# A two-block transformer kernel on one core: activations of the first block in rows of 512 columns, and feed-forward tiles at another place in SBUF

## The chip, the cores and the metric

The kernel runs on one core of one Trainium2 chip. The metric is device microseconds (us) of one execution. In the engines' names of the profile, PE is TensorE's matrix products, PEld its loads of the stationary operand, DVE is VectorE, ACT is ScalarE, POOL is GpSimd and SP is SyncE, which issues the weight transfers.

## The reference

512 tokens of 1024 channels go through two blocks, one after the other, in float32. Cut to what matters here:

```
# first block
h = x
h = h + 0.5 * swiglu(rmsnorm(h), ffn1_wg, ffn1_wu, ffn1_wd)   # 1024 -> 2816 -> 1024
u = rmsnorm(h) @ w_in                                         # queries, keys, values, gates
h = h + concat(rmsnorm(nsa(u)), rmsnorm(forgetting(u))) @ w_out
h = h + 0.5 * swiglu(rmsnorm(h), ffn2_wg, ffn2_wu, ffn2_wd)
h = h + sigmoid(rmsnorm(h) @ ple_w_gate) * rmsnorm(p @ ple_w_proj)
# second block: 16 meta tokens are put before the 512
h = concat(meta, h)
proj = rmsnorm(h) @ w_in_2                                    # nine parts of 1024
h = h + merged(hgrn2, gated convolution) @ w_out_2
a, val = split(rmsnorm(h) @ w_up_2)
h = h + (silu(causal_dwconv(a)) * val) @ w_down_2
out = rmsnorm(h)[16:]
```

## The kernel before

Channels lie on the 128 partitions and tokens in the free dimension. `KB` = 8 blocks of 128 channels make the width of 1024, and `FB` = 22 blocks the 2816 hidden channels, worked through in two halves of `HB` = 11. `T2` = 528 is the number of tokens with the meta tokens, `SEQ` = 512 without them.

**A product.** Every float32 operand is split into an upper part and a rest (names that end in h and l, or whi and wlo for weights), both of type float32r. `mm3` makes one block of a product as three instructions: upper times upper, upper weight times rest, rest of the weight times upper. The stationary operand is loaded by a load of its own (PEld) ahead of each product.

**Weights.** `Stream` brings weight chunks of 128 x 1024 in from HBM over SP's queue into `wraw`, and ACT and DVE split them into `whi` and `wlo`. `advance` keeps transfers and splits ahead of the products.

**Dense products.** `pieces_of` runs over the K blocks of one group of products: for each block k it takes 128 columns of a weight chunk as the stationary operand and the row `x[:, k]` of the activations, 512 tokens, as the moving one. In the feed-forward (`ffn`) a hidden block takes two groups of 8 K blocks, gate and up, with the activations of a `Norm` as moving operand. `down_proj` then takes for each of 8 output blocks 11 K blocks, with the hidden tiles `hh` and `hl` as moving operand. The moving operands of the first block are these: `X0` (`x0h`, `x0l`) in the first feed-forward, the output projection and the gate of the embedding; `X1` (`x1h`, `x1l`) in the second feed-forward; `hh` and `hl` in both down projections; `ph`, `pl` in the embedding's own projection. In the projections of the attention the roles are the other way round: 128 tokens of `X0` are stationary and 256 columns of weights move (288 in the first three chunks).

**Tiles.** `X0` and `X1` are tiles of 128 x 8 x 528 for the whole kernel. The first block uses the first 512 of the 528 columns of each row, the second block all of them, mostly in two products of 258 to 264 columns. `hh` and `hl` are taken from a pool that each feed-forward opens for itself. In the second feed-forward the pool gives two scratch tiles (`sq`) before them, since its norm's squares are summed ahead of it. Addresses follow from the order in which tiles are taken.

**Order.** Dense products are issued in program order. Side work (norms, splits, softmax) is issued between them by an estimate of the engines' clocks (`Clocks`). That estimate knows nothing of addresses. All instructions of the compute engines have the same line in the profile, L144, that of the wrapper `Engine`, so rows are told apart by their operands' names. Feed-forward groups write to PSUM banks `b` in the first block, and to `acc` and `h` in the second.

Where the tiles start within each partition of SBUF, taken from the built program of either version, as the remainder of a division by 512 bytes:

| operand | before | after |
|---|---|---|
| `whi`, `wlo`, 128 columns of block k (512 bytes each) | 160 | 160 |
| `x0h`, `x0l`, `x1h`, `x1l` in the first block, row k | 128 + 64 k | 160 |
| `hh`, `hl`, first and third feed-forward, any row | 160 | 160 |
| `hh`, `hl`, second feed-forward, any row | 288 | 160 |
| `ph`, `pl` | 160 | 160 |
| `x1h`, `x1l` in the second block, row k, first token | 128 + 64 k | 160 + 64 k |

Of the kernel before, what the change touches and what calls it, by code (L numbers as in the profile page):

```python
# [16 lines left out]
# The output leaves the meta tokens out: past the recurrence only the last two of them count, which a convolution looks  # L17
# back to, and two more before its own one. Products in two parts want both of them even.
# [6 lines left out]
HB = FB // 2  # L25
# [4 lines left out]
# groups of 256 columns of w_in, with their first columns, in the order of the attention's products  # L30
# [4 lines left out]
# column blocks of the per-channel parameters, in the order they are packed  # L35
# [12 lines left out]
# constants of the first block: cos, sin, causal, cmp mask, rows with a cmp block, head pick  # L48
# [9 lines left out]
class Clocks:  # L58
    """An estimate of when each engine is done with what was issued to it: it decides the order of issue only."""

    ENGINES = ("PE", "DVE", "ACT", "POOL")
    # from the end of an instruction to the start of one that depends on it
# [5 lines left out]
    def __init__(self):  # L68
        self.free = dict.fromkeys(self.ENGINES, 0.0)
        self.hop = {e: np.array([self.HOP.get((f, e), 200.0) for f in self.ENGINES]) for e in self.ENGINES}  # L70
        # per place: end of the last write and of the last read by each engine, for every 32 partitions and element
        self.marks, self.names, self.counts, self.index = {}, {}, {}, {}
        self.last = self.skip = 0.0
        self.dma = 2160.0
# [4 lines left out]
    def turn(self, ap, bufs):  # L79
        """A tile that takes one of `bufs` places in turns with others of its tag."""  # L80
        t = ap.tensor
        n = self.counts[t.tag] = self.counts.get(t.tag, -1) + 1
        self.names[t.name] = t.tag, n % bufs
        return ap
# [16 lines left out]
    def load(self, ap):  # L101
        """A transfer into a tile."""
        m, q, x = self.spot(ap)
        t = max(self.dma, m[:, :, q, x].max() + 1300)
        self.dma = t + 128 * 4 * _free_size(ap) / 360
        m[0, -1, q, x] = self.dma + 800
# [27 lines left out]
class Engine:  # L134
    """An engine whose instructions also move the estimate."""
# [55 lines left out]
class Slots:  # L191
    """Things used in turns (PSUM banks, scratch tiles), each with the estimated time from which it is free."""
# [9 lines left out]
    def get(self, keep=0, low=False):  # L202
        """A slot that is free by now, or None; `keep` of them stay for others."""
# [12 lines left out]
class Stream:  # L216
    """Weight chunks in the order in which they are used: loads run ahead of the split, the split ahead of the products."""
# [48 lines left out]
    def keep(self, j, pool):  # L266
        """The parts of chunk j have a place of their own."""
        self.kept[j] = pool

    def advance(self):  # L270
        """Split up to `ahead` chunks past the last one taken (`held`: taken ones that stay longer), keep the loads running."""
# [20 lines left out]
def build(tc, A, out):  # L292
# [9 lines left out]
    # ------------------------------------------------------------------ weight order  # L302
# [58 lines left out]
    # ------------------------------------------------------------------ what stays for the whole kernel  # L361
    h = base.tile([128, KB, T2], FT, name="h")
    X0 = (base.tile([128, KB, T2], FR, name="x0h"), base.tile([128, KB, T2], FR, name="x0l"))
    X1 = (base.tile([128, KB, T2], FR, name="x1h"), base.tile([128, KB, T2], FR, name="x1l"))
    ssq = base.tile([128, T2], FT, name="ssq")
    rB = base.tile([128, T2], FT, name="rB")
    rtok = base.tile([128, 5], FT, name="rtok")
# [14 lines left out]
    # ------------------------------------------------------------------ side work  # L382
    class Task:
        """Work beside the dense products, in stages: the next one is issued when the last one is done by the estimate."""
# [29 lines left out]
    def force():  # L414
        """Nothing can be issued now: go on to the next moment at which something is done."""
# [24 lines left out]
    class Store:  # L440
        """n tiles of one kind that are taken and given back."""

        def __init__(self, pool, name, n, shape, dt=FT):
            """pool: one for all of them, or a list with one for each."""
# [8 lines left out]
        def drop(self, ids):  # L453
            """Done with some of them."""
# [29 lines left out]
    def act(o, i, fn, exact=False, **kw):  # L484
        """ScalarE function with the table set chosen: Exp and Ln share one unless the logarithm has to be exact."""
# [8 lines left out]
    def mm3(ps, w, x, first, last):  # L494
        """hi*hi + hi*lo + lo*hi of one K block into each (psum, columns) pair."""
# [8 lines left out]
    def run(pieces, ev=None):  # L504
        """A group of products in pieces, with the side work between them; ev takes up the result."""
# [9 lines left out]
    def pieces_of(ps, w, x, ks=range(KB), first=0, last=KB - 1, step=1, off=0):  # L515
        """x: pair of tiles with K blocks, or a list of pairs, one for each K block."""
# [12 lines left out]
    # ------------------------------------------------------------------ rmsnorm  # L529
    def refine(r, v, t, wide=None):  # L530
        """r close to v**-0.5: one Newton step; the result may go, repeated, to a wider tile."""
# [9 lines left out]
    def rsqrt(r, v, t, wide=None):  # L541
        """In stages."""
# [6 lines left out]
    class Norm:  # L549
        """h * gain split into two parts, sums of squares on the side; the row factor rB comes after the products."""  # L550
# [41 lines left out]
    def wide_factors(src, n, dst, banks, pool, tag="sq"):  # L592
        """(mean over channels + eps)**-0.5 on every partition; the sum takes src in two parts."""
# [22 lines left out]
    def row_factors(src, n, r, banks, dst=None, keep_v=None):  # L616
        """(mean over channels + eps)**-0.5, tokens on partitions in r and, where it is asked for, on every partition."""
# [26 lines left out]
    # ------------------------------------------------------------------ gated feed-forward of the first block  # L644
# [7 lines left out]
    def ffn(norm, next_norm, pool, extra=None):  # L652
        n = SEQ
        hh = pool.tile([128, HB, n], FR, name="hh")
        hl = pool.tile([128, HB, n], FR, name="hl")
# [39 lines left out]
        for hf in range(2):  # L695
            for f in range(HB):
                g_ = banks.grab()
                if ws.i == 0:
                    # the first two groups side by side, as their K blocks come in
# [13 lines left out]
    # ================================================================== first block  # L713
# [7 lines left out]
    with tc.tile_pool(name="ffn1", bufs=1) as pool:  # L721
        n0 = Norm("ffn1_norm", META, SEQ, X0, pool)
        nmix = Norm("mix_norm", META, SEQ, X0, pool)
        table("silu_and_others")
        # products that nobody reads: TensorE has its full clock when the first loads are there
# [5 lines left out]
        # the first two chunks of weights come in halves  # L731
# [30 lines left out]
        ffn(n0, nmix, pool)  # L762
        drain()

    # ------------------------------------------------------------------ attention
    with tc.tile_pool(name="att", bufs=1) as pool:
# [16 lines left out]
        def place(dt):  # L783
            """First the windows of the compressed keys, then the outputs of the forgetting attention."""
# [18 lines left out]
        stack_tiles = [t[:, kb, :SEQ] for t in X1 for kb in range(KB)]  # L803
# [4 lines left out]
        def seen(*aps):  # L808
            """Condition: all of these have been written by now."""
            return lambda: all(M.written(a) <= M.now() for a in aps)  # L810

        # ---- values and gates, tokens on partitions
        def ev_aux(bs):
# [17 lines left out]
            # the gates are 1 / (1 + exp(-z))  # L831
# [8 lines left out]
            # log sigmoid(z) = min(z, 0) - log(1 + exp(-|z|)), the logarithm with its rounding put back  # L840
# [21 lines left out]
        def proj_aux():  # L862
            bs = [banks.grab() for _ in range(4)]
            k = 0
            for nk in (3, 3, 2):
                w = ws.get()

                def piece(k, i, w=w):
                    def f():
                        hi, lo = wk(w, i, 288)  # L870
                        for t in range(4):
                            c = slice(t * 128, (t + 1) * 128)
                            for n, (a, b) in enumerate(((X0[0], hi), (X0[0], lo), (X0[1], hi))):
# [6 lines left out]
        def gain_tables():  # L880
            # scores carry the sign -1/8, so that the row maximum is a minimum of what is stored
            for i, (n, f) in enumerate((("q_norm_nsa", -0.125), ("k_norm_slc", 1.0), ("k_norm_win", 1.0),
                                        ("q_norm_fox", -0.125))):
                V.tensor_scalar(cols[:, i:i + 1], pc(n), f, None, op0=OP.mult)
                if i < 3:
                    # the gains of the rotated channels are in the tables of the rotation
# [22 lines left out]
        def proj_half(ev):  # L909
            """256 columns, tokens on partitions; two token blocks share a bank, whose first product clears it for both."""  # L910
            bs = [banks.grab() for _ in range(2)]
            for wi in range(2):
                w = ws.get()

                def piece(k, i, w=w):
                    def f():
                        hi, lo = wk(w, i, 256)
                        for t in range(4):
                            c = slice(t * 128, (t + 1) * 128)
                            d = bs[t // 2].t[:, (t % 2) * 256:(t % 2) * 256 + 256]  # L920
                            for n, (a, b) in enumerate(((X0[0], hi), (X0[0], lo), (X0[1], hi))):
# [6 lines left out]
        # ---- queries and keys: norm and rotation with tokens on partitions, then channels on partitions  # L928
# [9 lines left out]
        def split_q(z, col, r):  # L938
            """Per head the two parts of q, one above the other."""
# [9 lines left out]
        def split_k(z, col, r):  # L949
            """Per head the upper part of k twice and the lower part twice."""  # L950
# [19 lines left out]
        def rotate(z, cos, sin, nh):  # L970
            """The first 16 channels of nh heads."""
# [13 lines left out]
        def qk_half(hz, tables, pairs):  # L985
            """tables: rotation of (first head, heads, table); pairs: what takes up each pair of heads."""
            def g(bs):
# [7 lines left out]
                # the row factor of the norm before cancels against this one, but for eps, which is scaled instead  # L995
# [68 lines left out]
        # ---- softmax attention, one unit = one head and 128 queries  # L1064
# [8 lines left out]
        def unit(u, hp):  # L1073
# [8 lines left out]
            if extra is not None:  # L1082
                # the forget sums of the keys; those of the query are the same along a row and leave its softmax as it is
# [35 lines left out]
        def user(ids, n):  # L1119
            """The slots `ids` are free again after n units have taken their scores."""  # L1120
# [34 lines left out]
        # 16 blocks of 64 keys and a window of 512 keys are all the keys there are, by the shapes alone: the selected and the  # L1155
        # window attention both go over all keys up to the query
        def nsa_units(j):
# [3 lines left out]
            for kind in range(2):  # L1161
                # two pairs of heads share a key: eight units each, twice
# [27 lines left out]
        # ---- compressed keys and values  # L1190
# [1054 lines left out]
```

## Time and profile before

| | |
|---|---|
| median of 3 runs | 2053.38 us (2053.29 to 2054.24) |
| span of the profiled execution, first to last instruction | 2052.2 us |
| PE busy | 2040.9 us, 99% of the span, 14058 instructions |
| PEld busy | 1807.5 us, 88% |
| DVE busy | 1208.6 us, 59% |
| ACT busy | 878.8 us, 43% |
| DMA, mean | 87 GB/s |

Of the profiled execution the trace has the span; what lies around it, as the difference to the median of the other runs, is 1.2 us. The chain of work that ended last is followed back from the last instruction, and its shares tell which engine set the end. A busy PE counts a product from its start to a modelled end, and products overlap; how fast they follow each other is read from a stretch's length over the number of products, or of weight loads, in it.

### The profile page before, as it was taken

The page shows a single profiled execution, that of the slowest core. Times are in us where ns is not written, and L with a number is a line of the kernel's source. Part 1 is how long each engine was busy: PE and PEld are TensorE (multiplying, and loading weights), DVE is VectorE, ACT ScalarE, POOL GpSimd, SP SyncE. Part 2 cuts the span into 40 slices and gives each one's busy share as a digit, 9 for nine tenths or more (in the row PEclk, how much of TensorE's full clock was granted, in tenths as well). Part 3 has the DMA queues.
Part 4 walks back from the last instruction along what each step waited for, and adds up shares of the span by engine and source line. Part 5 has one row for each costly group of instructions (what it writes and reads, how often), then busy time and mean ns, then how long its engine had stood idle before and what let it go on. Part 6 is the DMA issues. An engine that isn't in the chain of part 4 may idle for free.

```text
span 2052.2 us, 33936 instructions
## 1 busy us (share of the span) xinstructions
PE 2040.9 (99%) x14058; PEld 1807.5 (88%) x14058; DVE 1208.6 (59%) x2243; ACT 878.8 (43%) x1513; POOL 6.4 (0%) x17
## 2 busy tenths in 40 slices
PE   9999999999999999999999999999999999999998
PEld 7888888999997888888888999999999999888987
DVE  6433444678874844334458567666666766535554
ACT  5222223467767533223236444555546443222223
POOL 0000000000000000000000000000000000000000
PEclk9999999999999999999999999999999999999999
DMA  5223223332000422332232222222222232233222
GB/s 181 92 83 113 94 79 96 116 115 72 27 17 11 134 93 80 95 113 91 76 111 93 90 84 73 73 84 83 75 82 66 81 103 85 82 102 103 93 75 80
DMA packets 58170, 179.16 MB, mean 87 GB/s; under 512 B 7424, under 2 KB 9728, under 8 KB 58016
## 3 DMA queue, kind: packets, MB, share of 16 engines
q1 hardware_dynamic: 57648, 175.56, 27.3%
q8 instruction: 111, 1.82, 0.3%
q0 software_dynamic: 368, 1.42, 0.2%
q14 instruction: 43, 0.35, 0.1%
HBM read 174.86 MB, written 2.10 MB: 86 GB/s over the span
## 4 chain that ended last, share of the span: by engine, by line
PE 98%; DVE 1%; ACT 1%; DMA 0%; issue 0%; SPq 0%; DVEq 0%
PE b L144 58%; PE acc L144 28%; PE h L144 12%; DVE h L144 0%; DMA wraw<-in_ffn_wg 0%; ACT x1h L144 0%; ACT x1l L144 0%; DVE x1h L144 0%; DVE s L144 0%; ACT AT L144 0%; ACT whi L144 0%; DVE rd L144 0%; ACT L144 0%; ACT s L144 0%; DVE OA L144 0%
## 5 line engine op out<-in xcount | busy, mean ns | idle before, releaser
L144 DVE TENSOR_TENSOR wlo<-wraw,whi 128x1024 fp32r<-128x1024 f32 (+4 forms) x365 | 402.4, 1103 | 326.5 <-ACT whi L144 325.3
L144 ACT ACTIVATE whi<-wraw 128x1024 fp32r<-128x1024 f32 (+4 forms) x364 | 348.0, 961 | 431.0 <-PE h L144 138.5
L144 PE MATMUL acc<-x1h,whi 128*128 128x258 f32 (+2 forms) x1472 | 305.7, 289 | 0.0
L144 PE MATMUL acc<-x1l,whi 128*128 128x258 f32 (+2 forms) x1472 | 296.9, 283 | 0.0
L144 PE MATMUL acc<-x1h,wlo 128*128 128x258 f32 (+2 forms) x1472 | 296.8, 283 | 0.0
L144 PEld LDWEIGHTS acc<-x1h,whi 128*128 128x128 f32 x1472 | 228.5, 189 | 3.7
L144 PEld LDWEIGHTS acc<-x1l,whi 128*128 128x128 f32 x1472 | 228.4, 189 | 0.0
L144 PEld LDWEIGHTS acc<-x1h,wlo 128*128 128x128 f32 x1472 | 227.7, 189 | 0.0
L144 PE MATMUL b<-x0h,whi 128*128 128x512 f32 (+2 forms) x504 | 195.9, 391 | 0.2 <-DVE whi L144 0.2
L144 PE MATMUL b<-x0h,wlo 128*128 128x512 f32 (+2 forms) x504 | 195.2, 390 | 0.0
L144 PE MATMUL b<-x0l,whi 128*128 128x512 f32 (+2 forms) x504 | 195.2, 390 | 0.0
L144 PE MATMUL b<-x1l,whi 128*128 128x512 f32 (+1 forms) x368 | 142.2, 390 | 0.0
L144 PE MATMUL b<-x1h,wlo 128*128 128x512 f32 (+1 forms) x368 | 142.1, 390 | 0.0
L144 PE MATMUL b<-x1h,whi 128*128 128x512 f32 (+1 forms) x368 | 142.1, 390 | 0.0
L144 PE MATMUL b<-hh,wlo 128*128 128x512 f32 x352 | 137.9, 392 | 0.0
L144 PE MATMUL b<-hh,whi 128*128 128x512 f32 x352 | 137.9, 392 | 0.0
L144 PE MATMUL b<-hl,whi 128*128 128x512 f32 x352 | 137.9, 392 | 0.0
L144 ACT ACTIVATE hh<-u 128x512 fp32r<-128x512 f32 x66 | 41.7, 632 | 175.2 <-DVE u L144 175.2
L144 PEld LDWEIGHTS b<-x0h,whi 128*128 128x128 f32 x504 | 94.6, 189 | 22.0 <-ACT x0h L144 0.9
L144 PEld LDWEIGHTS b<-x0l,whi 128*128 128x128 f32 x504 | 95.0, 190 | 21.4 <-DVE x0l L144 0.3
L144 PEld LDWEIGHTS b<-x0h,wlo 128*128 128x128 f32 x504 | 94.6, 189 | 21.1 <-DVE wlo L144 0.3
L144 PE MATMUL b<-whi,x0h 128*128 128x256 f32 (+1 forms) x352 | 101.8, 289 | 0.3 <-DVE x1h L144 0.3
(371 smaller groups left out, 3545.1 us busy)
## 6 DMA issues: line engine op xcount, KB each, us to landing
wraw<-in_w_in SPq DMA_DIRECT2D x72, 512.0 KB, 3.6
wraw<-in_w_up SPq DMA_DIRECT2D x44, 512.0 KB, 3.5
wraw<-in_ffn_wg SPq DMA_DIRECT2D x43, 512.0 KB, 3.5
wraw<-in_ffn_wu SPq DMA_DIRECT2D x43, 512.0 KB, 3.5
wraw<-in_ffn_wd SPq DMA_DIRECT2D x32, 384.0 KB, 3.1
wraw<-in_ffn_wd SPq DMA_DIRECT2D x32, 320.0 KB, 2.9
wraw<-in_w_half SPq DMA_DIRECT2D x20, 512.0 KB, 3.6
wraw<-in_w_down SPq DMA_DIRECT2D x16, 384.0 KB, 3.0
```

The source lines that it names most:

```text
L144: r = f(*a, **k)
```

## The change

Four edits, apart from comments. `rtok`, a tile of 20 bytes, is taken from the pool before `X0` instead of after `rB`, which moves `X0`, `X1`, `ssq` and `rB` up by 32 bytes and nothing behind them. `Y0` and `Y1` are views of the same tiles as `X0` and `X1`, with rows of 512 columns one behind the other; all of the first block uses them in place of the tiles' first 512 columns. The second block keeps `X0` and `X1`. `hidden` takes `hh` and `hl` from the pool before anything else does.

```diff
     h = base.tile([128, KB, T2], FT, name="h")
+    rtok = base.tile([128, 5], FT, name="rtok")
     X0 = (base.tile([128, KB, T2], FR, name="x0h"), base.tile([128, KB, T2], FR, name="x0l"))
     X1 = (base.tile([128, KB, T2], FR, name="x1h"), base.tile([128, KB, T2], FR, name="x1l"))
+
+    Y0, Y1 = (tuple(t.rearrange("p k t -> p (k t)")[:, :KB * SEQ].rearrange("p (k t) -> p k t", k=KB) for t in x)
+              for x in (X0, X1))
     ssq = base.tile([128, T2], FT, name="ssq")
     rB = base.tile([128, T2], FT, name="rB")
-    rtok = base.tile([128, 5], FT, name="rtok")
...
-    def ffn(norm, next_norm, pool, extra=None):
+    def hidden(pool):
+        return pool.tile([128, HB, SEQ], FR, name="hh"), pool.tile([128, HB, SEQ], FR, name="hl")
+    def ffn(norm, next_norm, pool, hid, extra=None):
         n = SEQ
-        hh = pool.tile([128, HB, n], FR, name="hh")
-        hl = pool.tile([128, HB, n], FR, name="hl")
+        hh, hl = hid
...
-        n0 = Norm("ffn1_norm", META, SEQ, X0, pool)
-        nmix = Norm("mix_norm", META, SEQ, X0, pool)
+        hid = hidden(pool)
+        n0 = Norm("ffn1_norm", META, SEQ, Y0, pool)
+        nmix = Norm("mix_norm", META, SEQ, Y0, pool)
...
-        stack_tiles = [t[:, kb, :SEQ] for t in X1 for kb in range(KB)]
+        stack_tiles = [t[:, kb] for t in Y1 for kb in range(KB)]
...
-            run(pieces_of([(b.t, c512)], ws.get(), X0, range(4), 0, 3), ev_out(fb, b))
+            run(pieces_of([(b.t, c512)], ws.get(), Y0, range(4), 0, 3), ev_out(fb, b))
...
-        n2 = Norm("ffn2_norm", META, SEQ, X1, pool)
-        nple = Norm("ple_gate_norm", META, SEQ, X0, pool)
+        hid = hidden(pool)
+        n2 = Norm("ffn2_norm", META, SEQ, Y1, pool)
+        nple = Norm("ple_gate_norm", META, SEQ, Y0, pool)
...
-            run(pieces_of([(b.t, c512)], ws.get(), X0), ev_gate(fb, b))
+            run(pieces_of([(b.t, c512)], ws.get(), Y0), ev_gate(fb, b))
```

The other uses of `X0` in the first block (the projections of the attention, its normed outputs, the second half of the output projection) become `Y0` in the same way. On each engine the built program of the new version has the same instructions in the same order with the same waits as the one before: 12775 on PE, 2245 on DVE, 1467 on ACT, 21 on POOL and 389 on SP, and only addresses in SBUF differ.

## Rows read from the trace of the kernel before

**Rows 1.** The page: span, busy time of the engines, and the chain that ended last.

```profile
span 2052.2 us, 33936 instructions
PE 2040.9 (99%) x14058; PEld 1807.5 (88%) x14058; DVE 1208.6 (59%) x2243; ACT 878.8 (43%) x1513; POOL 6.4 (0%) x17
PE 98%; DVE 1%; ACT 1%; DMA 0%; issue 0%; SPq 0%; DVEq 0%
```

**Rows 2.** Waits of PE: who for whom, us in total, times, longest.

```profile
PE b L144 <- DVE onesr L144: 1.3, 1, 1.3
PE h L144 <- DVE fr L144: 1.3, 1, 1.3
```

**Rows 3.** Stretches of the down projections: length, PEld busy (loads), granted clock, DMA share, GB/s.

```profile
core 0: us, PEld busy (x), PEclk, DMA share, GB/s
131.43:191.28 59.85, 49.56 (x264) 1.00 0.34 105
314.48:374.33 59.85, 49.55 (x264) 1.00 0.34 99
828.09:889.43 61.34, 49.73 (x264) 1.00 0.33 103
1012.02:1073.36 61.34, 49.73 (x264) 1.00 0.35 103
1795.72:1855.58 59.86, 49.57 (x264) 1.00 0.35 105
```

**Rows 4.** Stretches of the first block's products with X0 or X1 moving; columns as before.

```profile
10.80:30.41 19.61, 15.78 (x84) 1.00 0.67 229
30.41:131.43 101.02, 81.68 (x436) 1.00 0.28 89
191.28:314.48 123.20, 99.38 (x528) 1.00 0.28 90
688.20:704.99 16.79, 13.55 (x73) 1.00 0.57 172
704.99:828.09 123.10, 99.52 (x530) 1.00 0.29 91
889.43:1012.02 122.59, 99.13 (x528) 1.00 0.28 91
1095.00:1129.85 34.85, 28.16 (x150) 1.00 0.29 92
```

**Rows 5.** Two stretches of Rows 4, one behind it: busy time of all engines.

```profile
core 0: us, PE busy (x) PEld busy (x) DVE busy (x) ACT busy (x) POOL busy (x), PEclk, DMA share, GB/s
191.28:314.48 123.20, 123.20 (x529) 99.38 (x528) 54.35 (x64) 34.95 (x43) 0.00 (x0) 1.00 0.28 90
1073.36:1129.85 56.49, 56.49 (x245) 45.82 (x244) 48.90 (x67) 36.63 (x55) 0.00 (x0) 1.00 0.29 94
```

**Rows 6.** Timeline of PE at the start: start us, modelled us, operands, shape.

```profile
9.23 0.63 PE L144 MATMUL b<-x0l,whi 128*128 128x512 f32 x1
9.66 0.63 PE L144 MATMUL b<-x0h,wlo 128*128 128x512 f32 x1
```

**Rows 7.** Stretches of 256 columns (attention), 65 columns, and 256 columns from hh.

```profile
389.75:404.06 14.31, 14.31 (x121) 1.00 0.29 87
610.29:613.54 3.25, 3.15 (x29) 1.00 0.00 0
2032.94:2035.81 2.87, 2.87 (x24) 1.00 0.00 0
```

**Rows 8.** Second block, stretches of 258, 258, 264 and 512 columns from X1.

```profile
1149.17:1166.45 17.28, 17.28 (x145) 1.00 0.41 122
1682.12:1687.90 5.78, 5.78 (x48) 1.00 0.39 107
1202.25:1207.56 5.31, 5.17 (x43) 1.00 0.16 59
1676.54:1682.12 5.58, 4.52 (x26) 1.00 0.17 65
```

**Rows 9.** Groups of PE by shape: operands, columns, count, busy us, mean ns.

```profile
L144 PE MATMUL acc<-x1h,whi 128*128 128x258 f32 x992 | 204.8, 288 | 0.0
L144 PE MATMUL b<-whi,x0h 128*128 128x256 f32 x320 | 92.3, 288 | 0.3 <-DVE x1h L144 0.3
L144 PE MATMUL acc<-x1h,whi 128*128 128x260 f32 x256 | 53.1, 289 | 0.0
L144 PE MATMUL acc<-x1h,whi 128*128 128x264 f32 x224 | 47.7, 294 | 0.0
L144 PE MATMUL acc<-x0h,whi 128*128 128x258 f32 x96 | 19.4, 283 | 0.0
```

More of the change, by code (lines that the diff above doesn't have):

```diff
@@ L761, in build @@
         spawn(squares(), 22e3)
-        ffn(n0, nmix, pool)
+        ffn(n0, nmix, pool, hid)
         drain()
@@ L872, in f @@
                             c = slice(t * 128, (t + 1) * 128)
-                            for n, (a, b) in enumerate(((X0[0], hi), (X0[0], lo), (X0[1], hi))):
+                            for n, (a, b) in enumerate(((Y0[0], hi), (Y0[0], lo), (Y0[1], hi))):
                                 P.matmul(bs[t].t[:, :288], a[:, k, c], b, start=k == 0 and n == 0,
@@ L920, in f @@
                             d = bs[t // 2].t[:, (t % 2) * 256:(t % 2) * 256 + 256]
-                            for n, (a, b) in enumerate(((X0[0], hi), (X0[0], lo), (X0[1], hi))):
+                            for n, (a, b) in enumerate(((Y0[0], hi), (Y0[0], lo), (Y0[1], hi))):
                                 P.matmul(d, a[:, k, c], b, start=k == 0 and n == 0 and t % 2 == 0,
@@ L1394, in out_norm @@
             dest[2].add(t)
-        na, normed = ((t[0][:, f:f + 4], t[1][:, f:f + 4], set()) for t, f in ((X0, 0), (X0, 4)))
+        na, normed = ((t[0][:, f:f + 4], t[1][:, f:f + 4], set()) for t, f in ((Y0, 0), (Y0, 4)))
         def nsa_norm(t):
@@ L1454, in build @@
             ws.held = fb
-            run(pieces_of([(half[fb][0].t[:, 256:], slice(256, 512))], half[fb][1], X0, range(4, 8), 4, 7, off=4))
+            run(pieces_of([(half[fb][0].t[:, 256:], slice(256, 512))], half[fb][1], Y0, range(4, 8), 4, 7, off=4))
         wait(lambda: len(normed[2]) == 4)
@@ L1477, in build @@
                 b, w = half[fb]
-                run(pieces_of([(b.t[:, :256], slice(0, 256))], w, X0, range(4, 8), 4, 7, off=4), ev_out(fb, b, n2))
+                run(pieces_of([(b.t[:, :256], slice(0, 256))], w, Y0, range(4, 8), 4, 7, off=4), ev_out(fb, b, n2))
                 ws.held = 0
@@ L1481, in build @@
             b = banks.grab()
-            run(pieces_of([(b.t, c512)], ws.get(), X0, range(4, 8), 4, 7, off=4), ev_out(fb, b, n2))
-        ffn(n2, nple, pool, lambda: (S.activation(ph, pr, AF.Copy), V.tensor_sub(pl, pr, ph.bitcast(FT))))
+            run(pieces_of([(b.t, c512)], ws.get(), Y0, range(4, 8), 4, 7, off=4), ev_out(fb, b, n2))
+        ffn(n2, nple, pool, hid, lambda: (S.activation(ph, pr, AF.Copy), V.tensor_sub(pl, pr, ph.bitcast(FT))))
         drain()
```

## Prediction

> **What bounds the kernel now.** I read the page first, then the waits, then stretches of equal products. The chain that ended last is PE for 98% of the span, and PE is busy for 99% of it [rows 1]. The longest waits of PE are 1.3 us each, one at the start and one at the end [rows 2]. So the time is how fast TensorE's products follow each other, and a change that leaves the instructions, their order and their waits as they are can act on the time only through that pace. The reader is to see it in stretches that hold nothing but one kind of product: length divided by the count of weight loads, one load for each product.
>
> The pace of products of 512 columns is not one number. The two down projections of the first feed-forward take 59.85 us for 264 products, 226.7 ns each; the two of the second take 61.34 us for 264, 232.3 ns; that of the third, in the second block, takes 59.86 us again [rows 3]. These five stretches have the same code, shapes, count and granted clock of 1.00, and nearly the same DMA share. What differs is where `hh` and `hl` begin: remainder 160, that of the weights, in the first and third, and 288 in the second. The products with `X0` or `X1` moving, whose rows begin at 128 + 64 k and so never at 160, go at 232.2 to 233.5 ns in every stretch [rows 4], like the down projections at 288. So the row says: 226.7 ns where the moving operand begins at the weights' remainder, and about 5.6 ns more, at the same clock, where it doesn't.
>
> **The change part by part.** No instruction is added, removed or moved on any engine or queue. I take 226.7 ns for every product of 512 columns in the first block that now begins at 160, and subtract stretch by stretch [rows 3, 4]:
>
> - First feed-forward, first half, as soon as products run at the full clock: 84 products in 19.61 us, 19.04 at the new pace, 0.57 us less; then 435 in 101.02 us (one load of the row's 436 belongs to the product after the edge), 98.61 at the new pace, 2.41 less.
> - Second half: 528 in 123.20 us, 119.70 at the new pace, 3.50 less.
> - Second feed-forward, first half: 530 loads in 123.10 us, two of them the norm's sum, so 528 products at 232.3 ns, 2.94 less. Second half: 528 in 122.59 us, 2.89 less.
> - Its two down projections, once `hh` and `hl` begin at 160: twice 61.34 − 59.85, 2.98 less.
> - Gate of the embedding: 150 in 34.85 us, 232.3 ns, 0.84 less; its other 42 products stand in the same stage and give 0.24 at the same difference. Together 1.09.
> - Output projection: 72 products in 16.79 us, 233.2 ns, 0.47 less; the 96 products of its first half, at the same 6.5 ns, 0.62. Together 1.09.
>
> Sum: 14.49 us from `X0` and `X1`, 2.98 us from `hh`, 17.47 us in all. The products ahead of 10.5 us follow each other 430 ns apart [rows 6], 1.2 columns in a ns, the lower of the clock's two levels (1.2 GHz); no row shows what an address does there, and I count nothing for the dozen of them.
>
> Two kinds of product change their addresses without becoming like those of rows 3. In the attention's projections the activations are stationary and 256 columns of weights move: 3 x 320 products [rows 9], at 119.2 ns (120 in 14.31 us) [rows 7]. Both operands now begin at 160. The nearest row that has this is the last down projection, 256 columns of `hh`: 24 in 2.87 us, 119.6 ns. A bound from below is the stretch of 65 columns, 28 in 3.25 us, 116.1 ns [rows 7]: a product of a quarter of the columns goes hardly faster, so the load of the stationary operand sets the pace here. I take the nearest row, 0.5 ns more with rounding, 0.5 us lost over 960 products; the bounds are 3.0 us gained (116.1 ns) and, by the nearest wider product, 258 columns at 120.4 ns (48 in 5.78 us) [rows 8], 1.2 us lost.
>
> In the second block `X0` and `X1` lie 32 bytes higher. Narrow products, 258 to 264 columns, are 3 x (992 + 256 + 224 + 96) = 4704 [rows 9]. Rows that start at 48 and 56 beyond a multiple of 64 go at 120.0 ns (144 in 17.28 us), those at 0 and 8 at 120.4 ns (48 in 5.78 us) [rows 8]. After the change these classes become 16 and 24, and 32 and 40, all of which keep what the old ones share, a first half on a multiple of 16 bytes and a second 8 bytes off it. I take no change, and 0.4 ns either way, 1.9 us, as the bound. The 528 products of 512 columns there go at 232.5 ns (24 in 5.58 us) from a remainder of 16 + 64 k [rows 8]; at 48 + 64 k they are still not at 160, so nothing is counted.
>
> What hides the rest: DVE is busy for 54.35 of 123.20 us and ACT for 34.95 in the densest stage that gets shorter, DMA for 0.28 [rows 5]. Losing 3.5 us leaves them far from the bound. The tightest stage is the embedding's, DVE 48.90 of 56.49 us [rows 5]; with 1.1 us less it is busy for 88%. If that cover were gone, what would be late is the group of products whose bank DVE has not yet emptied, at a cost of the 1.1 us that the stage gained at most.
>
> Net: 17.47 − 0.5 = 17.0 us. The span of 2052.2 us becomes 2035.2; the median of the runs lies 1.2 us above the span, so **2036.4 us**.
>
> A page speaks against this. The Trainium skill, SBUF — State Buffer, in its section on the two separate sides of SBUF, says that PE never waits on anyone for SBUF, and its table of paths gives the moving operand and the weight load read ports of their own. By that rule the remainder could not matter and the sum would be zero. The trace doesn't agree: 1.49 us between two stretches of 264 like products that differ in the address of one operand [rows 3]; I go by the rows.
>
> **The rivals.** (a) *The place of the activations doesn't work as that of `hh` does.* Only `hh` was seen at both remainders; `X0` and `X1` lie below the weights in a partition, `hh` above them, and eight different remainders of `X0` all give about 232 ns. For it: no row shows an activation of a `Norm` at 160. Against it: the pace at the wrong remainder is the same for `hh` and `X1`, 232.3 ns, which speaks for one mechanism. Then only the 2.98 us come, and 0.5 go: 2050.9 us. Halfway, with half of the 14.49 us, it is 2043.6 us.
>
> (b) *Addresses don't matter*, and the two paces of the down projections come from something else that differs between the feed-forwards, such as what DVE and ACT read and write beside them. That is the page's rule as a mechanism of this kernel. Against it stands that the third feed-forward, with other side work, goes at the pace of the first. Time: 2053.4 us, no change.
>
> (c) *Slower: the second block pays for the 32 bytes.* Its 4704 narrow products are tight to the weight load and more than those that gain. The dearest stretch of them is 264 columns, 42 in 5.31 us, 126.4 ns [rows 8]. If the new addresses bring all of them from 120.4 to that, 6.0 ns each, 28.2 us are lost and the time is 2064.6 us. It decides from 3.6 ns each, where the 17.0 us are used up. Against it: the two classes of starts in rows 8 differ by 0.4 ns, and part of those 126.4 is six more columns and other work between them.
>
> **How the numbers follow.** The forecast has a chance of 0.82: five stretches fix its price, and the layout after the change is that of `hh` in the first feed-forward, row for row. Halfway gets 0.07, (a) 0.04, (b) 0.04, (c) 0.03. The likeliest case's own range is 2036.4 − 3.5 (attention at 116.1 instead of 0.5 lost) − 1.9, that is 2031, up to 2036.4 + 0.7 (attention at 120.4) + 1.9 and 1.3 us for one new wait as long as PE's longest [rows 2], about 2040.5. It holds about 8 in 10, so it is the range. A measurement of this kernel can tell about 0.2%, 4.1 us, from no change. Faster by more than that: forecast and halfway, 0.89. Within: (a) and (b), 0.08. Slower: 0.03.
>
> **What the new profile would show.** Right: the second feed-forward's down projections take 59.85 us each, and the four stretches of 528 products about 119.7 us; the attention's projections stay within 1 ns of 119.2; the stretch of 48 products of 258 columns stays at 5.8 us; PE's waits stay as short as they are. Wrong by (a): the down projections get shorter and the 528 products stay at 122.6 to 123.2 us. By (b): no stretch moves. By (c): the first block gains and the second block, which starts 1129.85 us into the span now, takes over 17 us longer.

## The result

| | before | after |
|---|---|---|
| median of 5 runs | 2053.55 us (2053.29 to 2054.25) | 2038.27 us (2037.52 to 2039.51) |
| ratio, 95% interval | | 0.9924 [0.9913, 0.9934] |
| span of the profiled execution | 2052.2 us | 2037.7 us |

The change makes the kernel faster by 15.3 us by the medians; 17.0 were forecast. The spans of the two profiled executions differ by 14.5 us, since that of the changed kernel (2039.51 us) is the longest of its five. The page of the changed kernel has the same counts as [rows 1], DVE and ACT busy for as long as before, and the difference in PE.

```profile
span 2037.7 us, 33936 instructions
PE 2025.4 (99%) x14058; PEld 1807.2 (89%) x14058; DVE 1209.1 (59%) x2243; ACT 878.7 (43%) x1513; POOL 6.4 (0%) x17
```

The stretches of the down projections after the change, in the order and with the columns of [rows 3] (length, PEld busy and loads, granted clock, DMA share, GB/s):

```profile
129.99:189.82 59.83, 49.55 (x264) 1.00 0.35 105
309.50:369.34 59.84, 49.55 (x264) 1.00 0.34 99
820.47:880.31 59.84, 49.55 (x264) 1.00 0.36 106
999.99:1059.83 59.84, 49.55 (x264) 1.00 0.35 105
1780.96:1840.84 59.88, 49.55 (x264) 1.00 0.36 105
```

All five are alike now: the two in the middle went from 61.34 to 59.84 us. The stretches with `X0` or `X1` moving, which answer to [rows 4] (the fourth here is that of the second feed-forward's first half without its first 33 products):

```profile
31.36:129.99 98.63, 81.65 (x436) 1.00 0.29 91
189.82:309.50 119.68, 99.10 (x528) 1.00 0.31 93
683.94:700.28 16.34, 13.52 (x73) 1.00 0.62 176
708.24:820.47 112.23, 92.91 (x495) 1.00 0.30 90
880.31:999.99 119.68, 99.10 (x528) 1.00 0.30 93
1081.21:1115.22 34.01, 28.15 (x150) 1.00 0.32 94
```

119.68 us over 528 products is 226.7 ns, the pace of the down projections to the tenth of a ns. The attention's first stretch of 256 columns and three stretches of the second block, which answer to [rows 7, 8] (256, 258, 258 and 512 columns):

```profile
384.71:399.18 14.47, 14.47 (x121) 1.00 0.30 94
1134.56:1151.86 17.30, 17.30 (x145) 1.00 0.39 122
1667.10:1672.89 5.79, 5.79 (x48) 1.00 0.45 108
1661.51:1667.10 5.59, 4.51 (x25) 1.00 0.18 71
```

The attention's products lose 0.16 us in 120, and the second block's stay within 0.02 us of what they were.

### The profile page after: what moved, and what is told of

It reads as the page before. It is cut to its first block, busy times and chain, and to the rows that moved or that the text cites. A ratio compares the mean times of both kernels' runs of the same rounds, so it can differ in the third digit from the quotient of the medians.

```text
span 2037.7 us, 33936 instructions
## 1 busy us (share of the span) xinstructions
PE 2025.4 (99%) x14058; PEld 1807.2 (89%) x14058; DVE 1209.1 (59%) x2243; ACT 878.7 (43%) x1513; POOL 6.4 (0%) x17
## 4 chain that ended last, share of the span: by engine, by line
PE 98%; DVE 1%; ACT 1%; DMA 0%; issue 0%; SPq 0%; DVEq 0%
PE b L144 57%; PE acc L144 29%; PE h L144 12%; DMA wraw<-in_ffn_wu 0%; DVE h L144 0%; ACT x1h L144 0%; ACT x1l L144 0%; DVE x1h L144 0%; ACT AT L144 0%; DVE s L144 0%; DVE rd L144 0%; ACT L144 0%; ACT whi L144 0%; ACT s L144 0%; DVE OA L144 0%
```

## The experiments

Theory E, as in the prediction: a product's pace is set by where its two operands begin relative to each other. "Even" is said below of operands that begin at the same remainder. Rivals: what helps is that the rows lie a multiple of 512 bytes apart, or the address 160 itself, or the work beside the products. Runs with one execution are read by their stretches, not by their time, since the start of an execution moves by over 1 us (below).

**Only `hh` and `hl` first in their pools.** The kernel before, with `hid = hidden(pool)` ahead of the norms of either feed-forward, and nothing else of the change.

> The kernel before with one edit: hh and hl are taken from the pool first, so that they begin at 160 in the second feed-forward too; X0 and X1 as before. Theory E: its two down projections take 59.85 us each in place of 61.34, no other stretch moves, 2053.5 - 3.0 = 2050.5 us. Rival (the two paces come from the work beside the products): 61.34 us stay, 2053.5 us.

2051.46 us, against 2053.56 to 2056.36 for the kernel before, measured beside it. The second feed-forward's down projections, and the products of the first feed-forward's second half:

```profile
828.07:887.94 59.87, 49.55 (x265) 1.00 0.35 106
1011.14:1070.98 59.84, 49.57 (x264) 1.00 0.35 105
191.24:314.45 123.21, 99.38 (x529) 1.00 0.29 90
```

The 1.5 us a stretch come from addresses alone: DVE, ACT and DMA do the same work beside them, and that rival falls. One stretch didn't keep still as expected: the 528 products with `X1` between these two take 1011.14 − 887.94 = 123.20 us, where they took 122.59 before, with unchanged addresses of their own. Two things differ: what ran ahead of them, and where DVE and ACT write `hh` and `hl` beside them. The first half of the same feed-forward, beside which `hh` and `hl` are written at the new place too, keeps its 123.10 us:

```profile
704.97:828.07 123.10, 99.52 (x530) 1.00 0.29 91
```

That speaks for what ran ahead, in one pair of stretches; the run with the 32 bytes alone, below, shows no such difference.

**All rows at another remainder.** The changed kernel without its 32 bytes, so that `X0` and `X1` begin at 128 in every row:

```diff
     h = base.tile([128, KB, T2], FT, name="h")
-    rtok = base.tile([128, 5], FT, name="rtok")
...
     rB = base.tile([128, T2], FT, name="rB")
+    rtok = base.tile([128, 5], FT, name="rtok")
```

> The change without its 32 bytes: the rows of X0 and X1 in the first block are 2048 bytes apart, all at remainder 128, the weights at 160; hh and hl at 160 in all three feed-forwards. Theory E (the moving operand has to begin at the weights' remainder): the stretches of 528 products with X0 or X1 stay at the pace of before, about 232 ns, 122.5 us a stretch; the down projections of the second feed-forward have 226.7 ns; time about 2051 us. Rival U (what helps is that rows are a multiple of 512 bytes apart, wherever they begin): 226.7 ns, 119.7 us a stretch, time about 2038 us.

2052.07 us. Two stretches of 528 products with `X0` and `X1`, one of the second feed-forward's down projections, and the first of the attention:

```profile
192.12:315.33 123.21, 99.18 (x529) 1.00 0.28 90
888.45:1011.65 123.20, 99.19 (x528) 1.00 0.28 90
828.60:888.45 59.85, 49.55 (x264) 1.00 0.35 106
390.65:404.74 14.09, 14.09 (x121) 1.00 0.26 85
```

233.3 ns at 32 bytes below the weights, 226.7 for `hh` at their remainder. Rows at one remainder give nothing by themselves in these products.

**The 32 bytes alone.** The kernel before with `rtok` moved and the rows 2112 bytes apart.

> The kernel before with one edit, the 32 bytes: rows of X0 and X1 stay 2112 bytes apart and begin at 160 + 64 k, so that by a period of 256 bytes the K blocks 0 and 4 are at the weights' remainder, 1 and 5 at +64, 2 and 6 at +128, 3 and 7 at -64; hh of the second feed-forward stays at 288. Theory E, each product by its own distance: (226.7 + 228.9 + 232.3 + 233.3) / 4 = 230.3 ns on average, in the products with X0 or X1, 1.9 ns less than before, 2544 x 1.9 ns = 5 us less, the attention about as before: 2048.5 us. Rival (a whole group of products has to be even): 232 ns in all of them, 2053.5 us.

2053.07 us. The stretches of 528 products:

```profile
192.27:314.60 122.33, 99.17 (x528) 1.00 0.28 91
888.78:1011.12 122.34, 99.17 (x528) 1.00 0.28 91
```

231.7 ns, nearer to the rival's 232 than to the 230.3 that a price for each product by itself gives. A quarter of the products is even with its own weights, and there is hardly any gain. One group takes 8 blocks of channels with three products each, and the starts of all records show what becomes of the two even blocks, 0 and 4: their three products go on to the next after 226, 236 and 228 ns on average. Here is one such block, and the start of the product behind it:

```profile
922.16 0.39 PE L144 MATMUL b<-x1h,whi 128*128 128x512 f32 x1
922.38 0.40 PE L144 MATMUL b<-x1l,whi 128*128 128x512 f32 x1
922.62 0.39 PE L144 MATMUL b<-x1h,wlo 128*128 128x512 f32 x1
922.85 0.40 PE L144 MATMUL b<-x1h,whi 128*128 128x512 f32 x1
```

So a product's pace is not its own alone: an even product, in a block between uneven ones, can be as slow as they are. The down projections ahead of the two stretches went at 226.7 and 232.4 ns:

```profile
132.41:192.27 59.86, 49.55 (x264) 1.00 0.34 105
827.43:888.78 61.35, 49.73 (x265) 1.00 0.34 104
```

The stretches behind them are alike to 0.01 us, so here the pace ahead doesn't matter.

**The weights 256 bytes further.** The changed kernel with a pad ahead of the weights' pool:

```diff
     onesr = base.tile([128, 128], FR, name="onesr")
+    pad = base.tile([128, 64], FT, name="pad")
```

> The changed kernel with 256 bytes put before the weights' pool: weights, hh, hl, ph and pl begin at remainder 416, X0 and X1 in the first block stay at 160. Theory E with a period of 512 bytes: down projections keep 226.7 ns (59.85 us for 264), since they stay equal to the weights; products with X0 or X1 fall back to about 232 ns; time about 2038.3 + 14.5 = 2052.8 us, less than that if a distance of 256 costs less. Rival P (the period is 256 bytes): all keep 226.7 ns, 2038 us. Rival A (what counts is the address 160 itself, not that it is the weights'): X0 and X1 keep 226.7 ns, the three down projections go to about 232 ns, 2038.3 + 792 x 2 x 5.6 ns, about 2047 us.

2038.12 us. Products with `X0` at 160 and weights at 416, and a down projection with both at 416:

```profile
188.31:307.99 119.68, 99.10 (x528) 1.00 0.30 93
307.99:367.83 59.84, 49.55 (x264) 1.00 0.33 99
```

Neither moves: rival P. Operands 256 bytes apart go like even ones, so the period is 256 bytes, not 512. Rival A is out for the address 160 of 512, since `hh` keeps its pace at 416. By a period of 256, though, 416 is the same place as 160, and no run has weights and moving operand together at another place by 256. So it isn't shown that equality counts and not this one place; the wording of E is the simpler one, and no more.

**The lower parts of the weights 256 bytes further.**

```diff
-                hi, lo = (self.clocks.turn(self.pool.tile([128, 1024], FR, name=x, tag=x, bufs=b), b)
-                          for x in ("whi", "wlo"))
+                hi = self.clocks.turn(self.pool.tile([128, 1024], FR, name="whi", tag="whi", bufs=b), b)
+                if j == 0:
+                    self.pad = self.pool.tile([128, 64], FR, name="pad")
+                lo = self.clocks.turn(self.pool.tile([128, 1024], FR, name="wlo", tag="wlo", bufs=b), b)
```

> The changed kernel with 256 bytes between whi and wlo: whi begins at remainder 160, wlo at 416, X0 and X1 in the first block at 160, hh, hl, ph and pl at 416. Of three products in turn (whi with the upper part, whi with the rest, wlo with the upper part), those with X0 or X1 meet a load of whi at their own remainder, or of wlo 256 bytes off; those with hh the other way round. Theory L (a product's stream collides with the load that runs under it, which is that of the next product): with X0 the product of whi with the rest is slow (the load of wlo runs under it), the other two are at about 226.7 ns; with hh two of three are slow and that one is fast. Theory O (what counts is the product's own weights): with X0 the product with wlo is the slow one; with hh it alone is fast. In both the mean of three is about a third of the 5.6 ns above 226.7 with X0, two thirds with hh; time about 2038.3 + 14.5/3 + 1584 x 2/3 x 5.6 ns = 2049 us.

2039.31 us, and 119.68 us for 528 products with `X0` as before: with a period of 256 this pad changes nothing, so the run confirms the period and tells nothing of L and O.

**The same with 128 bytes** (`[128, 32]` in the pad).

> The changed kernel with 128 bytes between whi and wlo, now that 256 turned out to be a whole period: whi at 160, wlo at 288, X0 and X1 in the first block at 160 (whi's remainder), hh, hl, ph and pl at 288 (wlo's). Of three products in turn (whi with the upper part, whi with the rest, wlo with the upper part): theory L (a product's stream meets the load that runs under it, that of the next product): with X0 and X1 the product of whi with the rest is slow, the other two near 226.7 ns; with hh that one is near 226.7 ns and the other two slow. Theory O (the product's own weights count): with X0 and X1 the product with wlo is slow, with hh it alone is near 226.7 ns. In both the stretches with X0 or X1 go at about 228.6 ns on average and the down projections at about 230.5; time about 2038.3 + 2544 x 1.9 ns + 1584 x 3.8 ns = 2049 us. If neither holds and any unequal pair slows all three, they go at 232 ns.

2058.52 us. A stretch with `X0`, the down projection behind it, and a stretch with `X1`:

```profile
191.94:313.97 122.03, 99.87 (x528) 1.00 0.29 91
313.97:375.56 61.59, 49.59 (x264) 1.00 0.32 96
889.66:1011.69 122.03, 99.83 (x528) 1.00 0.30 91
```

231.1 and 233.3 ns, dearer than either theory said. Taken from the starts of all records of a kind in the first of these stretches, a product with `x0h` and `whi` goes on to the next after 226.7 ns, one with `x0l` and `whi` after 232.4, one with `x0h` and `wlo` after 234.3. L allowed only the second to be slow and O only the third; both are. With `hh` all three are slow, 233.0, 231.9 and 234.9 ns, the last of them though `hh` and `wlo` are even at another place (288). Both theories fall as they stood. What fits this run is that a product is quick where both its own weights and the next product's begin at the moving operand's remainder. In the run with the 32 bytes alone that fails: the product with `x1l` and `whi` in an even block has both, and takes 236 ns. So no rule for a single product came out. That `X0` kept its place and its products lost their pace shows at least that the moving operand's own place is not all that counts.

**Other distances.** The changed kernel with pads, one distance for each stage:

```diff
     rtok = base.tile([128, 5], FT, name="rtok")
+    pad0 = base.tile([128, 16], FT, name="pad0")
...
+    pad1 = base.tile([128, 8], FT, name="pad1")
     X1 = (base.tile([128, KB, T2], FR, name="x1h"), base.tile([128, KB, T2], FR, name="x1l"))
...
     onesr = base.tile([128, 128], FR, name="onesr")
+    pad2 = base.tile([128, 104], FT, name="pad2")
...
-    def hidden(pool):
+    def hidden(pool, n):
+        pool.tile([128, n], FT, name="pad3")
...
+        pool.tile([128, 96], FT, name="pad3")
         hh = pool.tile([128, HB, SEQ], FR, name="hh")
```

with `n` = 8 and 48 in the two feed-forwards of the first block.

> The changed kernel with small pads: the weights stay at 160, and the moving operands of the 512-column products begin at other distances from them, one for each stage: X0 +64 bytes, X1 in the first block +96, hh +32 in the first feed-forward, +192 in the second, -128 in the third. Theory E: each stage is above 226.7 ns, by an amount of its own; if any distance but 0 costs the same, all are near 232 ns and the time is near 2038.3 + 14.5 + 9 = 2062 us; if the cost grows with the distance, hh at +32 is the least. Rival A2 (the cost comes from single unlucky remainders): some of the five stay at 226.7 ns.

2053.89 us. In order: `X0` at +64, `X1` at +96, `hh` at +32, at +192 and at −128, and the first stretch of the attention:

```profile
191.24:312.10 120.86, 99.16 (x528) 1.00 0.28 92
886.88:1010.08 123.20, 99.11 (x528) 1.00 0.28 90
129.63:191.24 61.61, 49.49 (x265) 1.00 0.34 102
825.29:886.88 61.59, 49.37 (x264) 1.00 0.32 103
1793.06:1854.40 61.34, 49.74 (x265) 1.00 0.34 103
389.04:402.74 13.70, 13.70 (x121) 1.00 0.28 89
```

228.9 ns at +64, 232.3 at −128, 233.3 at the other three: every stage is above 226.7, as E said, and the cost doesn't grow with the distance. The time is 8 us below the estimate, in the main as +64 costs only 2.2 ns and because of the last row: the attention's 120 products, stationary operand 64 bytes above the moving one, follow each other at 114.2 ns, below the 116.1 ns of 65 columns [rows 7] that the prediction took for their floor.

**A place of its own for the attention's activations.** The changed kernel, with the norm ahead of the attention writing 64 bytes higher and the projections reading there:

```diff
+    Z0 = tuple(t.rearrange("p k t -> p (k t)")[:, 16:16 + KB * SEQ].rearrange("p (k t) -> p k t", k=KB) for t in X0)
...
-        nmix = Norm("mix_norm", META, SEQ, Y0, pool)
+        nmix = Norm("mix_norm", META, SEQ, Z0, pool)
...
-                            for n, (a, b) in enumerate(((Y0[0], hi), (Y0[0], lo), (Y0[1], hi))):
+                            for n, (a, b) in enumerate(((Z0[0], hi), (Z0[0], lo), (Z0[1], hi))):
```

> The changed kernel, but the norm ahead of the attention writes its rows of 512 columns 64 bytes higher (remainder 224), and the attention's projections read them there as stationary operand; everything else stays at 160. With the pads the same projections had X0 at this place and followed each other at 114.2 ns in their first stretch, against 120.6 ns after the change. Theory E (the relative place of the two operands sets the pace of these products too, with its own best distance): 120 products in 13.7 us in place of 14.47, and the stage from the projections to the output projection about 3.1 us shorter, as it was there; time 2038.3 - 3.1 = 2035.2 us. Rival B (the stage is bound by its softmax work on DVE and ACT, and shorter products only wait): the first stretch is shorter, the stage is not, 2038.3 us.

2035.02 us (2034.62 to 2035.26, 4 runs) against 2054.57 for the kernel before, measured beside it, ratio 0.9903 [0.9887, 0.9920]; that is also 3.2 us under the 2038.27 of the changed kernel. Its first stretch of the attention:

```profile
383.30:397.00 13.70, 13.70 (x121) 1.00 0.29 97
```

From the first product of the attention's projections to the first of the output projection it is 287.7 us, against 290.5 after the change (length, PE busy and products):

```profile
369.34:659.88 290.54, 289.53 (x2274) 1.00 0.19 57
367.96:655.65 287.69, 285.99 (x2274) 1.00 0.18 58
```

Among themselves the 256-column products save 3.8 us (by the starts of all that have another one right behind them), and the stage keeps 2.9 of it, so B falls. A new wait of PE in this stage, 0.5 us for DVE's `s`, is the part of B that is seen.

**Two more places**, 128 and 192 bytes higher (32 and 48 in place of 16).

> As the version with the attention's rows 64 bytes higher, but 128 bytes higher (remainder 288, the weights at 160). What is asked is whether 64 is one good distance among many or the only one. If any distance but 0 helps: 120 products in about 13.7 us (114 ns). If each distance has its own pace: between 116 and 121 ns, 13.9 to 14.5 us; time 2036 to 2038.5 us.

> The same with 192 bytes (remainder 352), which by a period of 256 is 64 below the weights. If what counts is how far apart the two are and not which comes first, 114 ns as at +64, 13.7 us for 120 products and 2035 us; if it counts which comes first, another pace, 116 to 121 ns, 13.9 to 14.5 us and 2036 to 2038.5 us.

2037.06 and 2036.29 us; the first stretch at +128 and at +192:

```profile
382.98:397.30 14.32, 14.32 (x122) 1.00 0.28 94
383.58:397.81 14.23, 14.23 (x121) 1.00 0.30 98
```

119.3 and 118.6 ns. With 120.6 at 0, 117.4 at −32 and 114.2 at +64, each of these distances has its own pace, and it counts which operand comes first: +192 is −64 by the period (with the weights 256 bytes further these products keep their 120.6 ns), and 4.4 ns dearer than +64.

## Why the prediction was right, and where a term was off

The mechanism was the one forecast, and rivals (a), (b) and (c) did not come: the activations gain as `hh` does, and the second block takes 922.5 us (from 1115.22 to the end of the span) where it took 922.3. Two of the signs that were named did not come: the attention's projections are 1.4 ns above 119.2, not within 1, and PE has a new wait of 0.9 us, at the start.

| step | forecast, us | measured, us |
|---|---|---|
| down projections of the second feed-forward | 2.98 less | 2 x (61.34 − 59.84) = 3.00 less |
| first feed-forward, second half | 3.50 less | 123.20 − 119.68 = 3.52 less |
| its first half, 435 products | 2.41 less | 101.02 − 98.63 = 2.39 less |
| second feed-forward, second half | 2.89 less | 122.59 − 119.68 = 2.91 less |
| gate, 150 products | 0.84 less | 34.85 − 34.01 = 0.84 less |
| output projection, the 72 products shown | 0.47 less | 16.79 − 16.34 = 0.45 less |
| attention's stage | 0.5 more | 290.5 − 289.6 = 0.9 more |
| start of the first feed-forward | 0.57 less | 25.5 (5.87 to 31.36) − 24.65 (5.76 to 30.41) = 0.8 more |

Three terms were mis-sized, by 1.4, 0.4 and 0.4 us, and with them the sum by some 2.3 us of the 2.5 that lie between the 17.0 forecast and the 14.5 of the two profiled spans. The start is the largest. In the timeline of the changed kernel PE waits 0.87 us for a split of ACT, goes on, and is at the full pace from 12.95 us (start us, modelled us, operands, shape, and the wait ahead):

```profile
7.04 0.50 PE L144 MATMUL b<-x0h,wlo 128*128 128x512 f32 x1
8.42 0.50 PE L144 MATMUL b<-x0h,whi 128*128 128x512 f32 x1 [0.87 <-ACT whi L144]
12.55 0.56 PE L144 MATMUL b<-x0l,whi 128*128 128x512 f32 x1
12.95 0.39 PE L144 MATMUL b<-x0h,wlo 128*128 128x512 f32 x1
```

After that wait the granted clock is 1.00 for another microsecond, and then 0.50, the lower level, for 3.4 us (length, PE busy and products, granted clock):

```profile
8.42:9.48 1.06, 1.06 (x4) 1.00 1.04 383
9.48:12.88 3.40, 3.40 (x9) 0.50 1.02 369
```

Before, PE had no wait for ACT there, and the full pace came at 10.83 us: 11 products in the 5.07 us ahead of it, against 14 in 7.08 now. At the later pace those would have taken 2.57 and 3.17 us, so the start costs 1.4 us more. The change is not the reason as far as the runs show. The changed kernel with its pads of 256 bytes, at the same paces in the stretches read above, reaches the full pace at 9.62 us in one profiled execution and at 12.62 in the other, and waits for `whi` 0.5 and 1.1 us; the kernel before with only `hh` and `hl` moved waits 0.6 us. The step took the profiled execution of before for the rule, where the moment differs by over 3 us from one execution to the next.

The attention's term was taken from 256 columns of `hh`, 119.6 ns; the stretch shows 120.6, at the dear bound of 120.4 and just past it. Its cheap bound, the floor read off 65 columns, was wrong as a reason: 114.2 ns were to be had at another distance. The prediction had the sign right and didn't see that the same edit could be a gain here if the stationary operand began elsewhere.

The output projection's first 96 products were priced like its other 72; the whole stage gave 0.7 us (41.06 to 40.4) in place of 1.09.

The step "where the moving operand begins at the weights' remainder" held, and two parts of its wording didn't: the remainder is by 256, and the price is not one of each product by itself. That it is the weights' remainder that counts, and not the place 160 by 256, was never put to the test, since the weights' upper part stood there in every run.

The Trainium skill, SBUF — State Buffer, on the two separate sides of SBUF, has PE wait on no one. If that were all, an address could not matter; in the run with `hh` alone it does, 59.84 against 61.34 us with nothing but addresses changed. No run here shows whether PE waits there for anyone, or for what.

## What to carry to other kernels

Where TensorE is busy all the time, read the pace of each stretch of equal products; two paces for one shape at one granted clock are a question about addresses. Put moving operands in rows that all begin at the stationary operand's remainder (by 256 bytes here, and seen at one such remainder only), and check the other way round apart: where activations are stationary the best distance was another. A difference of 5 ns in 230 is worth 15 us over 3000 such products, and it costs no instruction to save it.

## What the runs showed of the hardware that was not expected

The pace of 512 columns of float32r at a granted clock of 1.00 goes by how far the moving operand begins from the weights: 226.7 ns at 0 and also at 256 bytes, 228.9 at +64, 232.3 at 128, 233.3 at +32, −32, +96 and +192. In all these runs `whi` begins at 160 by 256. The last two figures may be one, since a stretch at unchanged addresses also moved by 1.2 ns (next).

The addresses of a product's own operands don't fix its pace. 528 products with unchanged addresses took 122.59 us behind a down projection at 232.3 ns and 123.20 us behind one at 226.7; with rows at 160 + 64 k it was 122.3 us behind either. In these last stretches a product with both operands at one remainder took 236 ns, in a block between uneven ones. What decides isn't shown.

Products of 256 columns ran at 114.2 to 120.6 ns by the distance alone, at the best below the 116.1 ns of 65 columns.

What TensorE waits for in the slower cases stays open. Two theories were tried, a collision with the load that runs under a product and one with its own weights, and neither gave the pattern of three that was measured.
